# Dilated attention on tokens kept in another order, and the norm vector loaded first

## The chip, the cores and the metric

One core of a Trainium2 chip runs the program. The metric is the device time of one execution in microseconds (us); lower is better. Engines: TensorE (PE; PEld is its weight load), VectorE (DVE), ScalarE (ACT), GpSimd (POOL) and SyncE (SP, which issues most DMAs; POOL issues stores). Each engine works through its own instructions in order.

## The reference

Two residual layers on 1024 tokens of width 1024, in fp32. Layer 1 joins grouped-query attention and a neighbourhood attention; layer 2 joins a gated delta-rule branch and the dilated attention that the change is about. Cut to what matters there:

```python
DILATED_PATTERNS = ((128, 1), (512, 4), (2048, 16))      # window, dilation

def dilated_pattern(q, k, v, rel_bias, window, dilation):
    # query t attends to keys t - j*dilation, j = 0..window/dilation, causal:
    # positions are split into `dilation` residue classes; within one, blocks of 128
    # queries see their own block of keys and the one before it
    scores = einsum(qb, kw) + bias[bucket(distance)]
    lse = logsumexp(scores); p = exp(scores - lse)
    return einsum(p, vw), lse

def dilated_attention_branch(qkv, gate, ...):             # 8 heads of 64
    outs, lses = the three patterns, each over rms-normed q and k
    o = sum(softmax(stack(lses)) * stack(outs))            # the union
    return o * silu(gate)

mixed = concat([y_dn, y_att]); return x + mixed @ w_out
```

## The kernel before

**Layers and streams.** `share` (L464) weaves two streams into one program: a main stream (attention, delta rule) and a fill stream (projections, output projection), whose matmuls are to stand where the main stream waits. A scheduler then fixes the order on each engine. Projections and score matmuls are done with operands split into a high and a low part (`whi`/`wlo`, `hh`/`hl`, `qh`/`ql`), three or two matmuls for one product.

**Start.** SP loads the first weights, eight tiles of x (`xt`, L560, raised in priority by `XPR`) and the norm vector `g8` (L553). TensorE transposes `g8` first, then the x tiles; ScalarE squares each x tile (L568), and evacuates the transposes, scaled by the vector, as `hh` (L589), VectorE the rest as `hl` (L590). From these the first projection starts.

**The dilated branch.** The fill stream projects q and k, v and the gate of a pair of heads j (0 to 3) to DRAM: `c_d[j]`, `cv_d[j]` and a part of `g2_d` (`proj_c`), token by token in natural order. `prep_c(j)` (L1527) loads q and k back (`lqk`), normalizes, transposes, and leaves k and q in SBUF with one token a column (`da0` to `da2`, or `k2`, `qh`, `ql`): 64 rows by 1024 columns for each head. `tables_c(j)` (L1520) loads the bias and mask tables from `rb_d`, which holds each head's bias expanded (stored by L1095, DRAM to DRAM, with an outermost count of 8): a DMA for each head and pattern.

`jobs_c(j)` (L1579) has 24 items a pair. `item` (L1591) issues, for 128 queries and the pair's two heads: four score matmuls (128x256; columns of q are the weights, columns of k move), on VectorE the custom addition of the table with the row's minimum (L1607), on ScalarE the exponential (L1609), on TensorE transposes (`s<-ident,Pc`), a copy to `PTc` (L1620), the matmuls with v (`po<-vc,PTc`), and on VectorE the copy into the result tile (L1630): `Nst` for dilation 4 and 16, `N0` for dilation 1. The items' order is eight of dilation 4, eight of dilation 16, eight of dilation 1:

```python
yield item(slice(c + 512 * n, c + 512 * n + 509, 4), slice(c, c + 512 * n + 509, 4), ...)   # dilation 4
yield item(slice(c, c + 1017, 8), slice(c, c + 1017, 8), ...)                              # dilation 16, two classes a tile
yield item(slice(i * 128, (i + 1) * 128), slice(max(i - 1, 0) * 128, (i + 1) * 128), ...)  # dilation 1
```

So the columns of q and k are 4, 8 and 1 elements (of 4 bytes) apart. Results of the first two patterns go to DRAM (`n_d[j][0]`, `n_d[j][1]`, by POOL, L1643 and L1650), and come back in token order.

**The union.** After items 4 and 8 of dilation 1, `union` (L1670) loads both other patterns' results of 512 tokens (`N`, L1675), takes the minimum over the patterns (`M`, L1678, L1679), the weights (`W`, `D`), loads the gate (`gtc`, L1693), merges and gates (L1699 to L1703) and has POOL store the result to `o2_d` (L1707); for the last pair it stays in SBUF (`od3`). There are eight unions in all.

**The end.** `first_part(2)` in the fill stream multiplies the seven first groups of 128 columns of the mixed rows with `w_out` and keeps sums in `yp_d` (L945 to L950). The last group, pair 3's, is done in `fill2` (L1151): each of eight tiles of `od3` is transposed (`mth`, `mtl`), multiplied, added (L1172) to what `yp_d` holds and stored.

Of the kernel before, what the change touches and what calls it, by code (L numbers as in the profile page):

```python
# [153 lines left out]
def hybrid_kernel(ctx: ExitStack, tc: tile.TileContext, A, out, dbg=None, upto=99):  # L154
# [102 lines left out]
    def rows(t, i):  # L257
        return t[i * 128:(i + 1) * 128]
# [283 lines left out]
    rb_d = dp.tile([8, 128, 1024], F32, name="rb_d")  # L542

# [6 lines left out]
    with tc.tile_pool(name="xp", bufs=2, reuse_waits="tile") as xp:  # L550

        g8 = xp.tile([8, 128], F32, name="g8", bufs=1)
        ld(g8, dram(A["norm_gain"], 0, [[128, 8], [1, 128]]))  # L553
# [236 lines left out]


# [121 lines left out]
    def put_mixed(M, i, k0, n, od, gd, to=None, buf=e5):  # L913
        r = (slice(i * 128, i * 128 + 128), slice(k0 * 128, (k0 + n) * 128))
        ot = buf()[:, 0:n * 128]
        ld(ot, od[r])
# [22 lines left out]
    def first_part(b, od, gd, w, src, dst, mk):  # L939

        def part(ks, src):
# [11 lines left out]
            for i in range(NT):  # L953
                put_mixed(M_, i, ks[0], len(ks), od, gd if ks[0] == 0 else None, buf=buf)
                yield 0.43
# [7 lines left out]
        yield from part(range(4), src)  # L963
        last_w.extend(out_w(w, range(LASTC[b], 8), c) for c in range(2))
# [156 lines left out]
    ab_d = [dp.tile([64, 256], F32, name="ab_d%d" % k) for k in range(4)]  # L1121
    tb_d = [dp.tile([64, 256], F32, name="tb_d%d" % k) for k in range(4)]


    def proj_c(j):
        def evac(i, p):
            sg = e5()
            S.activation(sg[:, 0:384], p[:, 0:384], AF.Copy)
            st(rows(c_d[j], i), sg[:, 0:256])
            st(rows(cv_d[j], i), sg[:, 256:384])  # L1130
            gate_out(p[:, 384:512], g2_d[i * 128:(i + 1) * 128, 512 + j * 128:512 + (j + 1) * 128], sg[:, 384:512])

        yield from proj_tok(H[2], w2, [(2056 + 128 * j, 512, 4, 128)], evac)
# [17 lines left out]
    def fill2():  # L1151
# [14 lines left out]
        for i in range(NT):  # L1166
            x = xx[i // 2][:, i % 2]
# [7 lines left out]
            yield from wait(("c", 3, i // 4))  # L1175
            to = tuple(wk.tile([128, 1, 128], F32R, name=n, bufs=2) for n in ("mth", "mtl"))
            put(to, slice(0, 128), od3[i // 4][:, i % 4].rearrange("p h d -> p (h d)"), 0, 1, 0.5)
# [342 lines left out]
    def tables_c(j):  # L1520
        Ts = [wk.tile([128, 2, w], F32, name="tab%d" % k, bufs=2) for k, w in enumerate((256, 256, 128))]
        for h in range(2):
            for k, T in enumerate(Ts):
                ld(T[:, h], dram(rb_d, (2 * j + h) * 131072 + 384 * k + 128, [[1023, 128], [1, T.shape[2]]]))
        return Ts

    def prep_c(j):  # L1527
# [22 lines left out]
        X[j] = k2, qh, ql, tables_c(j) if j else None  # L1550
        for b in range(0, NT, 4):
            ssq = sm.tile([128, 4, 4], F32, name="ssc", bufs=2)
            qk = []
            for i in range(0, 4, 2):
                qk += [tmp("lqk", 2 * LQ)]
                ld(qk[-1], c_d[j][(b + i) * 128:(b + i + 2) * 128].rearrange("(t p) (h d) -> p t h d", p=128, d=64))
# [5 lines left out]
            for i in range(b, b + 4):  # L1562
# [14 lines left out]
                yield 0.54  # L1577

    def jobs_c(j):  # L1579
# [5 lines left out]
        def values(n, *ap):  # L1585

            v = tile_c("vc")
            ld(v.rearrange("p t h d -> p (t h d)").rearrange("p (a b) -> p a b", a=n), dram(cv_d[j], 0, list(ap)))
            return [v[:, t] for t in range(8)]

        def item(q, k, vs, T, N, then=None):  # L1591
# [7 lines left out]
            for h in range(2):  # L1599
                kk = k2[:, h, k] if nkt == 2 else k2[:, :, k]  # L1600
# [5 lines left out]
            for h in range(2):  # L1606
                V.tensor_tensor_reduce(out=P[:, h, :nk], in0=sh[h], in1=T[:, h, T.shape[2] - nk:], op0=OP.add, op1=OP.min,  # L1607
# [29 lines left out]


        vs = values(2, [512, 128], [512 * 128, 2], [1, 512])
        for c in range(4):  # L1640
            N = nst()
            for n in range(2):
                then = (lambda N=N, c=c: st(dram(n_d[j][0], c * 132, [[4 * 132, 128], [512 * 132, 2], [1, 132]]), N)) if n else None  # L1643
                yield item(slice(c + 512 * n, c + 512 * n + 509, 4), slice(c, c + 512 * n + 509, 4),
                           [vs[c], vs[4 + c]][:n + 1], Ts[1], N[:, n], then)
        vs = values(1, [1024, 128], [1, 1024])
        for c in range(8):
            if c % 2 == 0:
                N = nst()
            then = (lambda N=N, c=c: st(dram(n_d[j][1], (c - 1) * 132, [[8 * 132, 128], [132, 2], [1, 132]]), N)) if c % 2 else None  # L1650
            yield item(slice(c, c + 1017, 8), slice(c, c + 1017, 8), vs[c:c + 1], Ts[2], N[:, c % 2], then)
        N0 = wk.tile([128, NT, 132], F32, name="N0")
        vs = values(8, [128, 128], [128 * 128, 8], [1, 128])
# [7 lines left out]
        for i in range(NT):  # L1661
            yield item(slice(i * 128, (i + 1) * 128), slice(max(i - 1, 0) * 128, (i + 1) * 128), vs[max(i - 1, 0):i + 1],
                       Ts[0], N0[:, i], (lambda b=i // 4: last(b)) if i % 4 == 3 else None)
# [5 lines left out]
    def union_c(j):  # L1669
        def union(N0, b):  # L1670

            Ns = [N0[:, 4 * b:4 * b + 4]]
            for p in range(2):
                N = tile_c("N%d" % (p + 1))
                ld(N, n_d[j][p][512 * b:512 * b + 512].rearrange("(t p) c -> p t c", p=128))  # L1675
# [11 lines left out]
            for p in (1, 2):  # L1687
# [5 lines left out]
            ld(gt.rearrange("p t h d -> p t (h d)"),  # L1693
               g2_d[512 * b:512 * b + 512, 512 + j * 128:640 + j * 128].rearrange("(t p) c -> p t c", p=128))
# [12 lines left out]
            st(dram(o2_d, 4 * b * 128 * 1024 + 512 + j * 128, [[1024, 128], [128 * 1024, 4], [1, 128]]), od.rearrange("p t h d -> p t (h d)"))  # L1707
# [59 lines left out]
```

## Time and profile before

| | us |
|---|---|
| median of 3 runs (lowest to highest) | 1679.88 (1677.62 to 1684.44) |
| the profiled execution | 1676.17 |
| its span | 1674.4 |

The granted clock was 0.976 of full speed over the span. Times in the rows count from the start of the span. A row of the timeline has its start, its length, engine, line, operation, output from inputs, shapes, and how many instructions of one kind were drawn together; in brackets stands the idle time of the engine before it, and what ended it. The dilated stage runs from about 1335 to 1645, the last output tiles after that.

### The profile page before, as it was taken

The page shows a single profiled execution, that of the slowest core. Times are in us where ns is not written, and L with a number is a line of the kernel's source. Part 1 is how long each engine was busy: PE and PEld are TensorE (multiplying, and loading weights), DVE is VectorE, ACT ScalarE, POOL GpSimd, SP SyncE. Part 2 cuts the span into 40 slices and gives each one's busy share as a digit, 9 for nine tenths or more (in the row PEclk, how much of TensorE's full clock was granted, in tenths as well). Part 3 has the DMA queues.
Part 4 walks back from the last instruction along what each step waited for, and adds up shares of the span by engine and source line. Part 5 has one row for each costly group of instructions (what it writes and reads, how often), then busy time and mean ns, then how long its engine had stood idle before and what let it go on. Part 6 is the DMA issues. An engine that isn't in the chain of part 4 may idle for free. (4 is left out here: it accounts for less than half of the span.)

```text
span 1674.4 us, 27776 instructions
## 1 busy us (share of the span) xinstructions
PE 1529.0 (91%) x9363; PEld 1345.6 (80%) x9363; DVE 1108.9 (66%) x3401; ACT 780.7 (47%) x2196; POOL 262.3 (16%) x475
## 2 busy tenths in 40 slices
PE   2988999999999989996799999998999979999996
PEld 2877788989898878884677788887888868788984
DVE  5569866666665554568546768577677677957646
ACT  6246445455454443544344443444443354566631
POOL 0000111212122212111100102122212011111122
PEclk9999999999999899998899999999999989999999
DMA  6321112331215797775344423314222375633475
GB/s 168 118 63 53 53 63 90 80 99 54 95 47 150 241 273 212 226 231 142 82 102 107 99 83 89 95 52 110 79 79 73 113 222 170 193 93 90 134 246 208
DMA packets 165738, 208.47 MB, mean 125 GB/s; under 512 B 23435, under 2 KB 119371, under 8 KB 165596
## 3 DMA queue, kind: packets, MB, share of 16 engines
q1 hardware_dynamic: 138476, 131.35, 29.0%
q0 software_dynamic: 27120, 75.36, 13.1%
q8 instruction: 74, 1.21, 0.3%
q14 instruction: 68, 0.56, 0.1%
HBM read 135.51 MB, written 75.32 MB: 126 GB/s over the span
## 5 line engine op out<-in xcount | busy, mean ns | idle before, releaser
L172 PE MATMUL pw<-whi,hh 128*128 128x512 f32 (+2 forms) x1032 | 358.4, 349 | 8.6 <-ACT whi L353 2.5
L172 PE MATMUL pw<-wlo,hh 128*128 128x512 f32 (+2 forms) x1032 | 356.9, 346 | 0.9 <-DVE wlo L354 0.9
L172 PE MATMUL pw<-whi,hl 128*128 128x512 f32 (+2 forms) x1032 | 355.5, 345 | 0.0
L172 PEld LDWEIGHTS pw<-whi,hh 128*128 128x128 f32 x1032 | 196.4, 191 | 31.6 <-ACT whi L353 4.4
L172 PEld LDWEIGHTS pw<-wlo,hh 128*128 128x128 f32 x1032 | 197.0, 191 | 20.0 <-DVE wlo L354 1.3
L172 PEld LDWEIGHTS pw<-whi,hl 128*128 128x128 f32 x1032 | 196.6, 190 | 20.1
L354 DVE TENSOR_TENSOR wlo<-e,whi 128x512 fp32r<-128x512 f32 (+3 forms) x168 | 103.2, 624 | 57.1 <-ACT whi L353 56.7
L172 PE MATMUL pw<-hh,whi 128*128 128x512 f32 x320 | 128.7, 402 | 11.2 <-ACT whi L353 10.8
L353 ACT ACTIVATE whi<-e 128x512 fp32r<-128x512 f32 (+3 forms) x168 | 95.2, 581 | 74.9 <-DMA e<-in_w_in_dram 59.9
L172 PE MATMUL pw<-hl,whi 128*128 128x512 f32 x320 | 126.4, 396 | 0.0
L172 PE MATMUL pw<-hh,wlo 128*128 128x512 f32 x320 | 125.0, 399 | 0.0
L172 PE MATMUL s<-k,qT 128*128 128x512 f32 (+1 forms) x282 | 89.3, 396 | 3.2 <-DVE rq_t L285 1.6
L172 PE MATMUL po<-vc,PTc 128*128 128x128 f32 x560 | 82.8, 283 | 4.0 <-DVE N L1630 3.1
L1607 DVE CUSTOM_DVE_ANT_0 Pc<-s,tab 128x128 f32<-128x128 f32 (+1 forms) x192 | 59.7, 348 | 39.8 <-PE s L172 34.6
L172 PEld LDWEIGHTS po<-vc,PTc 128*128 128x128 f32 x560 | 75.6, 198 | 8.5 <-DVE N L1630 4.8
L172 PEld LDWEIGHTS pw<-hh,whi 128*128 128x128 f32 x320 | 60.6, 189 | 25.9 <-ACT whi L353 13.9
L172 PE MATMUL po<-PT,vv 128*128 128x256 f32 x512 | 75.2, 286 | 1.1 <-ACT PT L774 0.6
L766 ACT ACTIVATE P<-s,nm 128x512 f32<-128x512 f32 x77 | 52.5, 685 | 45.8 <-DVE nm L763 41.6
L172 PEld LDWEIGHTS po<-PT,vv 128*128 128x128 f32 x512 | 67.9, 190 | 5.2 <-ACT PT L774 1.7
L1609 ACT ACTIVATE Pc<-Pc,Nst 128x128 f32<-128x128 f32 (+1 forms) x128 | 53.6, 421 | 35.5 <-DVE Nst L1607 25.0
L172 PEld LDWEIGHTS pw<-hh,wlo 128*128 128x128 f32 x320 | 60.3, 189 | 11.8
L172 PEld LDWEIGHTS pw<-hl,whi 128*128 128x128 f32 x320 | 60.5, 189 | 11.4
(422 smaller groups left out, 3530.0 us busy)
## 6 DMA issues: line engine op xcount, KB each, us to landing
e<-in_w_in_dram SPq DMA_DIRECT2D x72, 256.0 KB, 3.3
bq_d<-e POOLq DMA_DIRECT2D x32, 256.0 KB, 2.5
qT<-bq_d SPq DMA_DIRECT2D x32, 256.0 KB, 5.4
e<-in_w_out_dram SPq DMA_DIRECT2D x32, 256.0 KB, 3.9
xp_d<-mx POOLq DMA_DIRECT2D x32, 256.0 KB, 4.4
yp_d<-e POOLq DMA_DIRECT2D x32, 256.0 KB, 2.7
e<-in_w_in_dram SPq DMA_DIRECT2D x32, 192.0 KB, 3.6
raw_d<-e POOLq DMA_DIRECT2D x24, 256.0 KB, 2.4
```

Of the source, the lines that this page charges most:

```text
L172: self.last = f(*a, **k).ins
L353: S.activation(hi[:, :n], raw[:, :n], AF.Copy)
L354: V.tensor_tensor(lo[:, :n], raw[:, :n], f32(hi[:, :n]), op=OP.subtract)
L766: S.activation(P[:, hf * 512:(hf + 1) * 512], ss[hf], AF.Exp, bias=nm[:, 2:3], accum_out=den[:, h, hf:hf + 1])
L1607: V.tensor_tensor_reduce(out=P[:, h, :nk], in0=sh[h], in1=T[:, h, T.shape[2] - nk:], op0=OP.add, op1=OP.min, scale=-1.0, scalar=3e38, accu ...
L1609: S.activation(P[:, h, :nk], P[:, h, :nk], AF.Exp, bias=N[:, 128 + h:129 + h], scale=-1.0, accum_out=N[:, 130 + h:131 + h])
```

## The change

1. The load of `g8` gets a higher priority than those of x.
2. `c_d`, `cv_d` and the gate (now `gc_d`, of its own) are stored in another order of tokens, by `places`: a token's column is found from its number modulo 8 and so on, so that dilation 4 has columns 2 apart, dilation 16 contiguous ones, and dilation 1 columns 8 apart. `prep_c` and v's loads follow.
3. Whatever crosses between the orders by DMA uses `eighths`: four DMAs of 32 partitions with a DRAM side of [2][16][n] in place of one of 128 partitions. It is used for N, the gate, v of dilation 1, and the stores of the union (`oc_d`, of its own, in place of `o2_d`). `put_mixed` reads a tile's three groups from `oc_d` with three loads. A store of `n_d[j][0]` has an outermost count of 2 too.
4. The tables' rows and columns have to follow the order: `places_table` loads them in pieces (4 for dilation 1, 2 for each of the others, for each head), with the rows permuted by the DMA, into `nat`, and ScalarE copies blocks of 128 columns with the columns permuted (six a head). For pair 0 it is done in layer 1, kept in `tp_d` and loaded in one DMA.
5. The last eight output tiles come in the order 0, 4, 1, 5 and so on, each transposed by a matmul with the identity, its columns permuted.

Its core:

```diff
+        with tc.high_priority(2 * XPR):
+            ld(g8, dram(A["norm_gain"], 0, [[128, 8], [1, 128]]))
...
+    def places_table(j, h, k, nat, T):
+        w = 128 if k == 2 else 256
+        ds = ((4, 2, 16), (2, 16, 4), (16, 4, 2))[k]
+        f = (1023, 1023 * ds[0], 1023 * ds[0] * ds[1])
+        src = (2 * j + h) * 131072 + 384 * k + 128
+        if k == 2:
+            for z in range(2):
+                ld(nat[z::2, 0:w], dram(rb_d, src + f[2] * z, [[f[0], 16], [f[1], 4], [1, w]]))
+        else:
+            m = 128 // ds[0]
+            for x in range(ds[0]):
+                ld(nat[m * x:m * x + m, 0:w], dram(rb_d, src + f[0] * x, [[f[1], ds[1]], [f[2], ds[2]], [1, w]]))
+        for b in range(w // 128):
+            x4 = nat[:, 128 * b:128 * b + 128].rearrange("p (z y x) -> p x y z", x=ds[0], y=ds[1])
+            for d in (b, b + 2)[:2 if k == 0 and b == 0 else 1]:
+                S.activation(T[:, 128 * d:128 * d + 128].rearrange("p (x y z) -> p x y z", x=ds[0], y=ds[1]), x4, AF.Copy)
...
+    def places(t, i):
+        r = t.shape[1]
+        return dram(t, ((i >> 2) + 2 * (i & 3)) * r, [[8 * r, 16], [128 * r, 8], [1, r]])
+
+    def eighths(t, b, n):
+        r = t.shape[1]
+        return [(slice(32 * e, 32 * e + 32), dram(t, (b + 128 * e) * r, [[512 * r, 2], [8 * r, 16], [1, n]])) for e in range(4)]
...
-                yield item(slice(c + 512 * n, c + 512 * n + 509, 4), slice(c, c + 512 * n + 509, 4),
-                           [vs[c], vs[4 + c]][:n + 1], Ts[1], N[:, n], then)
+                def k(x, c=c):
+                    return x[:, 256 * c:256 * c + 256].rearrange("p (s n) -> p n s", n=2)
+                yield item(slice(256 * c + n, 256 * c + n + 255, 2), k, vs[2 * c:2 * c + n + 1], Ts[1][:, :, 128 - 128 * n:], N[:, n], then)
...
-            yield item(slice(c, c + 1017, 8), slice(c, c + 1017, 8), vs[c:c + 1], Ts[2], N[:, c % 2], then)
+            yield item(slice(128 * c, 128 * c + 128), None, vs[c // 2 + c % 2 * 4:][:1], Ts[2], N[:, c % 2], then)
...
-            yield item(slice(i * 128, (i + 1) * 128), slice(max(i - 1, 0) * 128, (i + 1) * 128), vs[max(i - 1, 0):i + 1],
-                       Ts[0], N0[:, i], (lambda b=i // 4: last(b)) if i % 4 == 3 else None)
+            def k(x, ks=ks):
+                return x.rearrange("p (s r) -> p r s", r=8)[:, ks]
+            yield item(slice(r, r + 1017, 8), k, vs[ks] if r else vs[0:1], T, N0[:, r], (lambda b=r // 4: last(b)) if r % 4 == 3 else None)
...
-                ld(N, n_d[j][p][512 * b:512 * b + 512].rearrange("(t p) c -> p t c", p=128))
+                for ps_, src in eighths(n_d[j][p], 4 * b, 528):
+                    ld(N[ps_].rearrange("p t c -> p (t c)"), src)
```

In the changed code lines move by up to 76: the addition of L1607 stands in L1670, the load of N in L1750, the gate's in L1769, the merge in L1774 to L1778, the output tiles' additions in L1222.

Three places of the engines' order. The first is ScalarE at the start, `sqrow` being the squares of the x tiles, `hh` the evacuations and `whi` the cast of weights. Before:

```order
L568 ACTIVATE sqrow,ssx<-xt 128x1024 x8
L353 ACTIVATE whi<-e_187 128x512
L589 ACTIVATE hh<-s,gT 128x256
L589 ACTIVATE hh<-pw,gT 128x256
L589 ACTIVATE hh<-s,gT 128x256
L589 ACTIVATE hh<-pw,gT 128x256
```

After:

```order
L570 ACTIVATE sqrow,ssx<-xt 128x1024 x6
L591 ACTIVATE hh<-s,gT 128x256
L591 ACTIVATE hh<-pw,gT 128x256
L570 ACTIVATE sqrow,ssx<-xt 128x1024
L591 ACTIVATE hh<-s,gT 128x256 x2
L591 ACTIVATE hh<-pw,gT 128x256 x2
L570 ACTIVATE sqrow,ssx<-xt 128x1024
```

Two evacuations now stand ahead of the seventh square and four more ahead of the eighth. The second place is SP at the second union of head pair 0; `lqk` and `nat` there belong to the preparation of the next pair, `e` to the output projection. Before:

```order
L1556 DMA lqk<-c_d_465 128x2x256
L1675 DMA N_15579<-n_d_0_470 128x4x132
L1556 DMA lqk<-c_d_465 128x2x256
L347 DMA e_16546<-in_w_out_dram 128x512
L1675 DMA N_15581<-n_d_1_471 128x4x132
L347 DMA e_17218<-in_w_out_dram 128x512
L1693 DMA gtc<-g_d 128x4x128
```

After:

```order
L808 DMA nat<-rb_d 32x1x256 x4
L808 DMA nat<-rb_d 64x1x256 x2
L1750 DMA N_15655<-n_d_0_471 32x1x528 x4
L1750 DMA N_15660<-n_d_1_472 32x1x528 x4
L1769 DMA gtc<-gc_d_495 32x1x512 x4
L1616 DMA lqk<-c_d_466 128x2x256
L808 DMA nat<-rb_d 32x1x256 x4
L808 DMA nat<-rb_d 64x1x256 x2
```

Three DMAs with others between them became twelve in a row, with table pieces on both sides. The third place is VectorE at the last union; `e` are the fill's last sums, `mtl` the low part of an output tile's transpose, `hl` and `hh` its additions. Before:

```order
L1678 TENSOR_TENSOR M<-N_17779,N_18073 128x8
L1630 COPY N_17779<-po 128x128
L1679 TENSOR_TENSOR M<-M,N_18075 128x8
L1682 TENSOR_TENSOR W<-M,N_17779 128x8
L1682 TENSOR_TENSOR W<-M,N_18073 128x8
L1682 TENSOR_TENSOR W<-M,N_18075 128x8
L312 SCALAR_TENSOR_TENSOR mtl<-pw,mth 128x128
L1686 TENSOR_TENSOR D<-W,N_17779 128x8
```

After:

```order
L1777 TENSOR_TENSOR od_18322<-od_18322,N_18301 128x512
L977 TENSOR_TENSOR e_17693<-pw,e_17693 128x512
L1778 TENSOR_TENSOR od_18322<-od_18322,gtc 128x512
L977 TENSOR_TENSOR e_17707<-pw,e_17707 128x512
L977 TENSOR_TENSOR e_17721<-pw,e_17721 128x512
L977 TENSOR_TENSOR e_17735<-pw,e_17735 128x512
L977 TENSOR_TENSOR e_17749<-pw,e_17749 128x512
L1233 SCALAR_TENSOR_TENSOR mtl<-pw,mth 128x128
L1222 TENSOR_TENSOR hl<-pw,hl 128x512 x2
```

The union stood between the output tiles, behind the last of the fill's sums; it now stands among those sums, and all output tiles behind both.

## Rows read from the trace of the kernel before

**Rows 1.** The page's engines: busy us, share of the span, instructions.

```profile
PE 1529.0 (91%) x9363; PEld 1345.6 (80%) x9363; DVE 1108.9 (66%) x3401; ACT 780.7 (47%) x2196; POOL 262.3 (16%) x475
```

**Rows 2.** Windows; columns: length, busy by engine as named, clock, DMA share, GB/s.

```profile
core 0: us, PE busy (x) PEld busy (x) DVE busy (x) ACT busy (x) POOL busy (x), PEclk, DMA share, GB/s
0.00:30.00 30.00, 4.96 (x21) 4.17 (x21) 12.26 (x56) 15.56 (x30) 0.20 (x4) 1.00 0.82 195
...
1335.00:1645.00 310.00, 286.78 (x1717) 257.06 (x1716) 215.55 (x860) 169.39 (x584) 43.66 (x72) 0.97 0.52 166
...
1640.00:1674.00 34.00, 20.91 (x95) 13.66 (x93) 22.34 (x52) 3.04 (x10) 9.19 (x17) 0.97 0.62 221
```

**Rows 3.** Timeline of TensorE, score matmuls by four: dilation 4, 16, then 1.

```profile
1335.05 1.29 PE L172 MATMUL s<-da,da 128*128 128x256 f32 x4
...
1374.45 1.30 PE L172 MATMUL s<-da,da 128*128 128x256 f32 x4
...
1422.51 0.74 PE L172 MATMUL s<-da,da 128*128 128x256 f32 x4
...
1428.76 0.72 PE L172 MATMUL s<-da,da 128*128 128x256 f32 x4
```

**Rows 4.** Timeline of SyncE: the norm vector's load.

```profile
8.99 0.34 SPq L553 DMA_DIRECT2D g<-in_norm_gain_dram  x1
```

**Rows 5.** Timeline of TensorE at the start; in brackets: idle before, its end.

```profile
23.28 0.27 PE L172 MATMUL po<-ident,g 8*128 8x8 f32 x1 [4.09 <-DMA g<-in_norm_gain_dram]
...
32.56 1.09 PE L172 MATMUL s<-ident,xt 128*128 128x128 f32 x4 [7.96 <-DVE hl L590]
```

**Rows 6.** Timeline of ScalarE at the start.

```profile
24.71 1.06 ACT L568 ACTIVATE sqrow<-xt 128x1024 f32<-128x1024 f32 x1 [1.55 <-DMA xt<-in_x_dram]
...
26.28 0.45 ACT L589 ACTIVATE hh<-s,gT 128x256 fp32r<-128x256 f32 x1
```

**Rows 7.** Timeline of TensorE at the entry to the dilated stage.

```profile
1350.64 1.57 PE L172 MATMUL s<-ident,Pc 128*128 128x128 f32 x6 [6.55 <-ACT Pc L1609]
```

**Rows 8.** Timeline of VectorE at the entry to the dilated stage.

```profile
1342.63 0.69 DVE L920 TENSOR_TENSOR e<-e,e 128x512 f32<-128x512 f32 x1
...
1349.28 0.28 DVE L1607 CUSTOM_DVE_ANT_0 Pc<-s,tab 128x128 f32<-128x128 f32 x1
```

**Rows 9.** Timeline of VectorE in the tail.

```profile
1639.85 0.69 DVE L949 TENSOR_TENSOR e<-pw,e 128x512 f32<-128x512 f32 x1 [1.67 <-PE pw L172]
...
1648.72 0.17 DVE L1678 TENSOR_TENSOR M<-N,N 128x8 f32<-128x8 f32 x1 [1.09 <-DMA N<-n_d]
...
1657.45 0.69 DVE L1703 TENSOR_TENSOR od<-od,gtc 128x512 f32<-128x512 f32 x1
...
1668.04 1.40 DVE L1172 TENSOR_TENSOR hh<-pw,hh 128x512 f32<-128x512 f32 x2 [0.80 <-PE pw L172]
```

**Rows 10.** Line L1273 on ScalarE: ns min/median/max.

```profile
L1273 ACT ACTIVATE sq_d<-orr x32: 292/310/356, 1037.3 to 1343.1; 128x128 f32<-128x128 f32 x32
```

**Rows 11.** DMA issues from 1335 to 1645: count, KB each, median us to landing.

```profile
vc<-cv_d SPq DMA_DIRECT2D x12, 512.0 KB, 4.2
...
N<-n_d SPq DMA_DIRECT2D x16, 264.0 KB, 3.5
...
tab<-rb_d SPq DMA_DIRECT2D x16, 128.0 KB, 3.1
gtc<-g_d SPq DMA_DIRECT2D x8, 256.0 KB, 3.4
```

**Rows 12.** The tile N: ns that SyncE takes to issue a load.

```profile
L1675 SPq DMA_DIRECT2D N<-n_d x16: 360/370/387, 1379.7 to 1643.3; - x16
```

**Rows 13.** Window with the store of the expanded tables (L1095) alone; columns as rows 2.

```profile
62.00:66.00 4.00, 4.00 (x35) 4.00 (x35) 3.35 (x20) 0.83 (x3) 0.00 (x0) 1.00 0.53 216
```

**Rows 14.** Waits between 1354 and 1590: us in total, times, longest.

```profile
DVE M L1679 <- DMA N<-n_d: 6.0, 4, 2.1
```

More of the change, by code (lines that the diff above doesn't have):

```diff
@@ L542, in hybrid_kernel @@
     rb_d = dp.tile([8, 128, 1024], F32, name="rb_d")
+    tp_d = dp.tile([128, 2, 768], F32, name="tp_d")
     w1 = A["w_in"][0]
@@ L915, in put_mixed @@
         ot = buf()[:, 0:n * 128]
-        ld(ot, od[r])
+        if isinstance(od, list):
+            for k, t in enumerate(od):
+                ld(ot[:, k * 128:k * 128 + 128], places(t, i))
+        else:
+            ld(ot, od[r])
         if gd is not None:
@@ L963, in first_part @@
         yield from part(range(4), src)
+        if b == 1:
+            for h in range(2):
+                for k, (a, z) in enumerate(COLS):
+                    nat, T = (wr.tile([128, w], F32, name=n, bufs=2) for n, w in (("nat", 256), ("tabp", 384)))
+                    places_table(0, h, k, nat, T)
+                    st(tp_d[:, h, a:z], T[:, 0:z - a])
         last_w.extend(out_w(w, range(LASTC[b], 8), c) for c in range(2))
@@ L1165, in fill2 @@
         xx = [wn.tile([128, 2, 1024], F32, name="hh" if k % 2 else "hl", bufs=2) for k in range(4)]
-        for i in range(NT):
-            x = xx[i // 2][:, i % 2]
+        for r in range(NT):
+            i = (r >> 1) + 4 * (r & 1)
+            x = xx[r // 2][:, r % 2]
             ld(x, rows(yp_d, i))
@@ L1173, in ev2 @@
                 st(out[i * 128:(i + 1) * 128, c * 512:c * 512 + 512], y)
-            yield from wait(("c", 3, i // 4))
+            yield from wait(("c", 3, r // 4))
             to = tuple(wk.tile([128, 1, 128], F32R, name=n, bufs=2) for n in ("mth", "mtl"))
-            put(to, slice(0, 128), od3[i // 4][:, i % 4].rearrange("p h d -> p (h d)"), 0, 1, 0.5)
+            tb = wbank()
+            PE.matmul(tb[:, 0:128], od3[r // 4][:, r % 4].rearrange("p h d -> p (h d)"), ident.rearrange("p (e c a) -> p a c e", e=4, c=2),
+                      start=True, stop=True)
+            hv, lv = (t[:, 0] for t in to)
+            S.activation(hv, tb[:, 0:128], AF.Copy, scale=0.5)
+            V.scalar_tensor_tensor(lv, tb[:, 0:128], 0.5, f32(hv), op0=OP.mult, op1=OP.subtract)
             yield 0.22
@@ L1520, in tables_c @@
     def tables_c(j):
[L1521 to L1525, printed above, removed]
+        T = wk.tile([128, 2, 768], F32, name="tab", bufs=2)
+        if j == 0:
+            ld(T, tp_d)
+        else:
+            nat = wk.tile([128, 2, 640], F32, name="nat")
+            for h in range(2):
+                for k, (a, b) in enumerate(COLS):
+                    places_table(j, h, k, nat[:, h, 256 * k:], T[:, h, a:b])
+        return [T[:, :, a:b] for a, b in COLS]
     def prep_c(j):
@@ L1606, in item @@
             for h in range(2):
-                V.tensor_tensor_reduce(out=P[:, h, :nk], in0=sh[h], in1=T[:, h, T.shape[2] - nk:], op0=OP.add, op1=OP.min,
+                V.tensor_tensor_reduce(out=P[:, h, :nk], in0=sh[h], in1=T[:, h], op0=OP.add, op1=OP.min,
                                        scale=-1.0, scalar=3e38, accum_out=N[:, 128 + h:129 + h])
@@ L1636, in nst @@
             return tile_c("Nst")
-        vs = values(2, [512, 128], [512 * 128, 2], [1, 512])
+        vs = values(4, *[(slice(64 * e, 64 * e + 64), dram(cv_d[j], 512 * e * 128, [[256, 64], [128 * 128, 4], [1, 256]])) for e in range(2)])
         for c in range(4):
@@ L1706, in union @@
                 return
[L1707 removed]
+            for ps_, dst in eighths(oc_d[j], 4 * b, 512):
+                st(dst, od[ps_].rearrange("p t h d -> p (t h d)"))
         return union
```

41 lines of the change are left out of this document (24 added, 17 removed).

## The prediction

> **What bounds the kernel now.** I read the page's table of engines first: TensorE is busy 1529.0 us of 1674.4, VectorE 1108.9 [rows 1]. So what the change does to TensorE counts nearly in full, and other engines' work counts only where TensorE stands still. Next the windows, because the edits lie in three stretches [rows 2]: in the first 30 us TensorE does 4.96 us of work; in the dilated stage, 1335 to 1645, it does 286.78 of 310.00 us, the granted clock is 0.97 and the DMA engines are 0.52 busy; from 1640 to the end it does 20.91 of 34.00. The stage therefore moves with TensorE's own work, the two ends with their chains of waits. The sum is made against the profiled execution, 1676.17 us, which is 3.7 below the median of the runs, 1679.88. About 0.5%, 8.4 us, is what a measurement can tell from no change, so the marks are 1671.5 and 1688.3.
>
> **Score matmuls with other strides.** An item issues four score matmuls of 128x256. With columns a stride of 4 or 8 apart the group of four takes 1.29 and 1.30 us, with contiguous columns 0.74 and 0.72 [rows 3]. A stride of 4 is 16 bytes, one of 8 is 32: they cost the same. There are 8 items of each pattern in each of 4 head pairs, so 32 groups a pattern. Before: 32 contiguous, 32 at stride 4, 32 at stride 8. After: 32 at stride 8, 32 at stride 2, 32 contiguous. So two of the three classes trade places, and the whole gain hangs on the price of stride 2, 8 bytes, which the trace of before does not show. Its bounds are the two rows: 1.29, gain 0; 0.72, gain 32 x 0.57 = 18.2 us. I take the lower price, since 8 bytes is nearer to 4 than to the 16 at which the dear price has already been reached. TensorE is busy 93% of the stage [rows 2], and a shorter matmul gives its time only where the next one's data are there, but the fill's matmuls stand between the items: **-18**, ends -18.2 and 0. The Trainium skill (SBUF — State Buffer, Specifications) says lines of SBUF are 16 bytes and want two hits each for full bandwidth. By it stride 2 (two hits) would have the low price and stride 4 (one) the high one; the rows on strides 4 and 8 agree, and no row shows stride 2.
>
> **The norm vector first.** SP issues g at 8.99, behind the eight x loads [rows 4]; TensorE's first instruction waits 4.09 us for it [rows 5], and all transposes stand behind it. ScalarE then makes the last tile's square at 24.71, after a wait of 1.55 for that tile, and the first evacuation only at 26.28 [rows 6]. After the change g is ahead of the x loads, and six of the sixteen first evacuations stand ahead of the eighth square. Gain: the wait of 4.09 less what then waits for x instead; the evacuations can fill the 1.55 and what ScalarE lost to the late start. I take **-3.5**; ends 0 (the x tiles, 0.82 of the DMA engines' time in this window [rows 2], are late anyway) and -8, the 7.96 us that TensorE later stands for VectorE [rows 5].
>
> **Entry to the dilated stage.** TensorE stands 6.55 us until the first items' exponentials come [rows 7]; VectorE reaches the first of its additions at 1349.28, and at 1342.63 it still does fill work of 0.69 us a piece [rows 8], four pieces until then. In the new order that work stands earlier, and pair 0's table comes in one load, from rows that layer 1 prepared, in place of six. Three of the pieces lie on the chain: **-2**; ends 0 and -6.5.
>
> **The tail.** Before, the fill's last addition is at 1639.85, the second union of pair 3 waits for its loads at 1648.72, ends with the gate at 1657.45, and four output tiles follow, the last at 1668.04 [rows 9]: some 29 us, of which TensorE works 20.91 in the window of 34.00 [rows 2]. After, the union's merge and gate stand among the fill's last nine additions, four of them behind the gate, so its chain runs beside fill matmuls, and the eight tiles come in one run. The tiles' pace is 2.5 us: from the gate, 1657.45, to the end of the last addition, 1668.04 + 1.40, are 12.0 us, of which 2.0 go to the gate itself and an earlier pair of additions, and the other 10 to four tiles. Eight tiles and some 4 us before them make 24: **-5**; ends 0 and -8. The new transposes (a matmul by a permuted identity) have the shape of the old ones and are costed at nothing.
>
> **Tables on ScalarE.** Pairs 1 to 3 load their tables in natural row order and ScalarE copies 128x128 blocks with permuted columns: 12 a pair, 36 in the stage. The nearest row is an activation of 128x128 at 0.31 us [rows 10]: 36 x 0.31 = 11 us. ScalarE has room, but the copies come in bursts (up to 11 in a row in its order) between exponentials for which TensorE waits; a burst of 11 is 3.4 us. Three pairs with about 1.3 each that is not covered: **+4**; ends 0 and +11. The 12 copies in layer 1 lie beside projections, at nothing; without that cover they would add 12 x 0.31 = 4.
>
> **Loads that few DMA engines carry.** N comes in 64 DMAs of 66 KB in place of 16 of 264, the gate in 32 of 64 KB in place of 8 of 256, the third pattern's v in 16 of 128 KB in place of 4 of 512; one quarter of the tables in four pieces [rows 11]. SP issues some 129 DMAs more from the first table load on, at 0.37 us each [rows 12], 48 us of its queue over 310, which has that room. The rows get longer (2112 bytes in place of 528), so fewer packets. Against that, the DRAM side of each such DMA has an outermost count of 2. The trace has a store whose outermost count is 8: while it runs alone, the DMA engines are 0.53 busy at 216 GB/s [rows 13], that is half of the 16, at 216 / (16 x 0.53) = 25.5 GB/s each. If the outermost count sets how many engines work, two carry 51 GB/s. The Trainium skill (DMA: Bandwidth & Descriptors, Why a DMA increments its semaphore by 16 and not by 1) says so: the count of engines is the largest number up to 16 that divides both sides' slowest dimension. The row of the store with 8 agrees; no row shows a count of 2.
> Worked out for a pair: N 16 x 67.6 KB = 1081, gate 524, v 524, tables 262, together 2.39 MB; at 51 GB/s 47 us in the 78 us that a pair lasts (about 310 / 4). That fits, if the queue is not asked all at once. It is asked at a union: N 541 KB and gate 262 take 10.6 + 5.1 = 16 us instead of some 6 (two landings of 3.5 and 3.4 [rows 11] with their issues). VectorE now waits 6.0 us in four waits at the minimum over N [rows 14]; I take about one us more at each of the eight unions: **+9**. Ends: -6 (the waits go) and +40 (rival A). The stores of N and of the results go through POOL, whose queue the 24 result stores lengthen by 18; nobody waits for those but the late out-projection, so nothing.
>
> **Sum.** -18 - 3.5 - 2 - 5 + 4 + 9 = -15.5: 1676.17 - 15.5 = 1660.7, and with the 3.7 to the median 1664.4; I say **1665**, own range 1655 to 1675.
>
> **Rivals.**
> A, slower: the two engines become the bound. Place: the minimum over N at the second union of each pair, on VectorE, with the copies and additions of the next pair's items queued behind it and TensorE waiting for those. Price: the full 16 - 6 = 10 us at each of 4 second unions, 40, in place of my 9, so 31 more, of which some 4 in the last pair fall beside fill matmuls: 1665 + 27 = 1692. It decides if VectorE reaches the minimum less than 16 us after N's first load could start. For it: outermost count 2 in the diff, 0.53 in the row with count 8, and SP's order, where both N, the gate and table pieces follow each other. Against it: the 0.52 of DMA time in the stage leaves the queue room, and the four waits at the minimum come to only 6.0 us now. By the rule of the Trainium skill named above (DMA: Bandwidth & Descriptors) two engines it would be. Chance 0.20.
> B, the few engines cost nothing: the loads of four pieces spread, rows of 2112 bytes go faster than those of 528, and the waits at N vanish. In place of +9 about -2: 1654. For it: only 0.52 of the DMA time is used. Against it: the row with count 8. Chance 0.20.
> C, the change does not do what it says to the matmuls: stride 2 is as dear as stride 4, and the -18 is 0: 1665 + 18 = 1683, say 1682. For it: strides of 4 and 8 don't differ, so it may be contiguous or not that counts. Chance 0.15.
>
> **How the numbers follow.** Forecast 0.45, A 0.20, B 0.20, C 0.15. Faster by over 0.5%: four fifths of the forecast (0.36) and all of B, 0.55 in round numbers; within: the rest of the forecast, nearly all of C and a little of A, 0.25; slower: most of A, 0.20. The range runs from 1647, which holds most of B (1654 with some us below for a start at its end of -8), to 1692, the middle of A: left out are half of A and a third of B at most, under 0.2.
>
> **What would show it.** In the profile of the changed kernel: score groups of the dilation-16 pattern 0.72, of dilation 4 0.72 (C: 1.29), of dilation 1 1.29; TensorE's first instruction before 20 us; N's landing 3 to 5 us (A: 10 or more) and the waits at the minimum over N under 20 us in sum (A: 40). If the dilated stage is not some 10 us shorter while TensorE's work in it has fallen by 18, the loads or the bursts on ScalarE ate it, and the prediction's two added terms are too small. If TensorE's work has not fallen, it is the price of stride 2.

## The result, and the profile after

The changed kernel takes 1796.38 us (median of 4 runs, 1793.74 to 1802.39) against 1682.16 of the kernel before on the same chip: ratio 1.0671, 95% interval 1.0644 to 1.0698, some 114 us slower. The forecast of 1665 us and its whole range are wrong; the sign too. Below, differences in us between runs are differences of their ratios to the kernel before, times its 1684 us.

The page's engines and the windows of the kernel after (columns as in [rows 2]):

```profile
PE 1567.8 (87%) x9371; PEld 1374.7 (77%) x9371; DVE 1107.8 (62%) x3401; ACT 798.0 (44%) x2244; POOL 280.0 (16%) x499
...
0.00:30.00 30.00, 7.23 (x29) 5.56 (x29) 13.20 (x57) 17.39 (x34) 0.20 (x4) 1.00 0.82 194
```

```profile
1367.00:1797.00 430.00, 321.64 (x1748) 277.73 (x1748) 222.15 (x854) 178.94 (x610) 65.50 (x105) 0.88 0.39 124
...
1686.00:1689.00 3.00, 0.00 (x0) 0.00 (x0) 0.00 (x0) 0.00 (x0) 0.00 (x0) 0.50 0.13 52
1689.00:1692.00 3.00, 0.00 (x0) 0.00 (x0) 0.00 (x0) 0.00 (x0) 0.00 (x0) 0.50 0.13 52
```

From the first exponential's transposes to the end it takes 430 us where the kernel before took 324 (1350.64 [rows 7] to its span's end, 1674.4), with nearly as many instructions and a granted clock of 0.88. That is 106 us; some 17 more in these two profiles lie before it. The last two rows show what happens: no compute engine works, the clock has gone down to its lower level of 1.2 GHz, and the DMA engines are 0.13 busy at 52 GB/s. 0.13 of 16 is two engines. The timeline of TensorE and that of SyncE at that place, and long waits after 1330 (columns as in [rows 14]; the last two rows are the kernel before):

```profile
1694.91 0.48 PE L172 MATMUL pw<-ident,e 128*128 128x128 f32 x1 [13.62 <-DMA e<-oc_d]
```

```profile
1676.18 3.58 SPq L1651 DMA_DIRECT2D vc<-cv_d  x4
1679.94 2.45 SPq L942 DMA_DIRECT2D e<-oc_d  x2
1682.53 3.83 SPq L1750 DMA_DIRECT2D N<-n_d  x2
1695.42 0.56 SPq L942 DMA_DIRECT2D e<-oc_d  x1
```

```profile
PE pw L172 <- DMA e<-oc_d: 24.3, 4, 13.6
...
DVE M L1753 <- DMA N<-n_d: 18.2, 4, 6.1
...
DVE M L1754 <- DMA N<-n_d: 13.3, 4, 5.0
...
DVE M L1679 <- DMA N<-n_d: 8.2, 6, 2.1
DVE M L1678 <- DMA N<-n_d: 1.1, 1, 1.1
```

The waits at the minimum over N, 9.3 us before (6.0 of them in the window of [rows 14]), are 31.5 now. The single longest, 13.62, is for a load of `oc_d` whose own outermost count is 16, the first of the two issued from 1679.94 on: it lands late in a stretch in which two engines work off a backlog.

The trace also keeps every update of the semaphore that counts a load's landing. A load of N in the kernel before has sixteen. In the changed kernel it has one, 1.0 us after its issue, and then two, for example both at 3.5 us (issue at 1382.61); in the run runs16b below, where its outermost count is 8, it has one and then eight. So with an outermost count of 2 or 8 as many engines report. N lands after 6.1 us in the median, 13.8 at most; before it was 3.5. The load of `oc_d` issued at 1679.94 has sixteen updates: fourteen between 2.5 and 2.9 us, the other two only at 14.5 and 14.9. So TensorE stood for two of its sixteen engines.

The score matmuls after, by four, of dilation 4, 16 and 1 (against [rows 3]):

```profile
1376.68 1.17 PE L172 MATMUL s<-da,da 128*128 128x256 f32 x4
...
1397.28 0.72 PE L172 MATMUL s<-da,da 128*128 128x256 f32 x4
...
1411.13 1.29 PE L172 MATMUL s<-da,da 128*128 128x256 f32 x4
```

Dilation 16 and 1 changed places as forecast, but stride 2, now dilation 4's, costs 1.17, not 0.72.

### The profile page after: what moved, and what is told of

Same layout as the page of the kernel before. It is cut to its first block, busy times and chain, and to the rows that moved or that the text cites. A ratio compares the mean times of both kernels' runs of the same rounds, so it can differ in the third digit from the quotient of the medians.

```text
span 1796.7 us, 28066 instructions
## 1 busy us (share of the span) xinstructions
PE 1567.8 (87%) x9371; PEld 1374.7 (77%) x9371; DVE 1107.8 (62%) x3401; ACT 798.0 (44%) x2244; POOL 280.0 (16%) x499
## 4 chain that ended last, share of the span: by engine, by line
issue 37%; PE 27%; DMA 19%; POOL 7%; DVE 5%; ACT 2%; SPq 1%; POOLq 0%; DVEq 0%; ACTq 0%
PE pw L172 17%; PE s L172 6%; DMA n_d<-Nst 3%; DMA N<-n_d 3%; PE po L172 2%; DMA e<-oc_d 2%; DMA gtc<-gc_d 2%; PE p L172 2%; POOL g_d L524 1%; DMA e<-in_w_in_dram 1%; DMA nat<-rb_d 1%; DMA e<-in_w_out_dram 1%; POOL o_d L648 1%; DMA e<-yp_d 1%; DMA xt<-in_x_dram 1%
## 5 line engine op out<-in xcount | busy, mean ns | idle before, releaser
L172 PE MATMUL pw<-whi,hh 128*128 128x512 f32 (+2 forms) x1032 | 363.2, 353 | 12.5 <-DVE e L977 7.0
L172 PE MATMUL pw<-wlo,hh 128*128 128x512 f32 (+2 forms) x1032 | 361.0, 350 | 0.1
L172 PEld LDWEIGHTS pw<-whi,hh 128*128 128x128 f32 x1032 | 200.2, 195 | 35.6 <-DVE e L977 7.7
L172 PEld LDWEIGHTS pw<-whi,hl 128*128 128x128 f32 x1032 | 200.3, 194 | 20.6
L172 PEld LDWEIGHTS pw<-wlo,hh 128*128 128x128 f32 x1032 | 200.7, 194 | 19.9 <-DVE wlo L354 0.6
L172 PE MATMUL po<-vc,PTc 128*128 128x128 f32 x560 | 91.8, 304 | 28.0 <-DVE Nst L1693 13.7
L172 PEld LDWEIGHTS po<-vc,PTc 128*128 128x128 f32 x560 | 83.3, 216 | 34.1 <-DVE Nst L1693 15.9
L172 PE MATMUL s<-ident,Pc 128*128 128x128 f32 x280 | 62.1, 309 | 30.5 <-ACT Pc L1672 29.9
L1670 DVE CUSTOM_DVE_ANT_0 Pc<-s,tab 128x128 f32<-128x128 f32 (+1 forms) x192 | 59.3, 348 | 40.5 <-PE s L172 29.6
L172 PEld LDWEIGHTS s<-ident,Pc 128*128 128x128 f32 x280 | 40.6, 159 | 39.6 <-ACT Pc L1672 36.8
```

Of the source, the lines that this page charges most:

```text
L172: self.last = f(*a, **k).ins
```

## The experiments

**Engines or the number of DMAs.** Two runs on the changed kernel.

```diff
-        return [(slice(32 * e, 32 * e + 32), dram(t, (b + 128 * e) * r, [[512 * r, 2], [8 * r, 16], [1, n]])) for e in range(4)]
+        return [(slice(32 * e, 32 * e + 32), dram(t, (b + 256 * e) * r, [[8 * r, 32], [1, n]])) for e in range(4)]   # four16
...
+        return [(slice(0, 128), dram(t, b * r, [[8 * r, 128], [1, n]]))]                                           # one16
```

> Two theories for the 114 us that the change added. Engines: a DMA whose DRAM side has an outermost count of 2 runs on two engines, so N, the gate, v and the results land late. Queue: it is the number of DMAs on SyncE, each 0.6 us to issue and, by the waits of SyncE in the changed kernel (8.5 us on a load of the same tile), held until an earlier one has landed. Here the four DMAs stay four, with the same bytes and row lengths, but their DRAM side is one run of 32 strided rows instead of 2 times 16 (other rows than the right ones, so the merged values are of the wrong tokens). Engines: below 1715. Queue: 1780 to 1800, no change.

> One DMA of 128 partitions in place of the four, for N, the gate, v and the results (again rows of other tokens). Engines: the same as with four DMAs on many engines, within 5 us. Queue: here, and only here, the time falls, to below 1715. Both theories leave some 10 to 30 us over the kernel before, for the tables and the results' loads.

Measured: 1.0173 (1.0138 to 1.0209) and 1.016 (1.012 to 1.0199). Four DMAs with the same bytes, but an outermost count of 32, take away 84 of the 114 us, and one in place of four adds nothing to that that can be told. The engines, then: in four16 a load of N has sixteen updates of its semaphore, and lands after 2.4 us in the median. SyncE's side of it, the tile N in the kernel after, in four16 and in one16 (ns to issue one load, min/median/max):

```profile
L1750 SPq DMA_DIRECT2D N<-n_d x64: 583/616/2172, 1382.6 to 1732.1; - x64
```

```profile
L1750 SPq DMA_DIRECT2D N<-n_d x64: 302/419/1512, 1381.8 to 1652.7; - x64
```

```profile
L1750 SPq DMA_DIRECT2D N<-n_d x16: 319/325/402, 1404.1 to 1666.7; - x16
```

Even the issue of a DMA with an outermost count of 2 is longer, 616 ns against 419.

**The tables, alone and with that.**

```diff
-                    places_table(j, h, k, nat[:, h, 256 * k:], T[:, h, a:b])
+                ld(T[:, h, a:b], dram(rb_d, (2 * j + h) * 131072 + 384 * k + 128, [[1023, 128], [1, b - a]]))
```

> The changed kernel with the tables loaded as before, six DMAs a pair, no copies on ScalarE and none of the preparation in layer 1 (the table's rows and columns are then in the wrong order). Engines: 36 of the 64 pieces are of two engines, 32 KB each, and the 48 copies take 0.43 us each: 10 to 20 us less, 1775 to 1785. Queue: 40 DMAs fewer at 0.6 us, and what is queued behind them: 25 to 40 less, 1755 to 1770. If the tables cost nothing: 1790 to 1800.

> The two edits of the earlier runs together: one DMA for N, the gate, v and the results, and the tables as before. If the costs add, 1710 - 16 = 1694, some 10 over the kernel before. If the tables' 16 us were mostly their two-engine pieces' place in SyncE's queue, which one16 has already relieved, more than 1700.

Measured: 1.0571 (1.053 to 1.0612), 17 us less than the changed kernel; with one16, 1.0103 (1.0062 to 1.0144), 10 less than one16. By the intervals each difference is known to some 8 to 10 us, so that the two may be the same. In the profiles about half of it lies in the stage, counted from the first exponential's transposes to the end: 429.3 us against 421.6 without these tables, and 349.3 against 340.1 with one16. Part of the rest lies in layer 1, where the changed kernel prepares pair 0's tables and ScalarE waits for their pieces (columns as in [rows 14], between 590 and 660):

```profile
ACT tabp L813 <- DMA nat<-rb_d: 24.4, 5, 10.2
```

TensorE's 3700th to 3900th matmuls, which are issued there, take 40 to 46 us in the four profiles of kernels with this preparation (after, four16, one16, fix16), and 34 to 37 in those without it, the kernel before among them. (Of the pieces, 32 have an outermost count of 2, not the 36 of the expectation.)

**The stores of dilation 4's results.** The prediction had put them at nothing.

```diff
-  st(dram(n_d[j][0], 128 * c * 132, [[512 * 132, 2], [2 * 132, 64], [1, 264]]), N.rearrange("p n c -> p (n c)"))
+  [st(dram(n_d[j][0], (128 * c + 512 * e) * 132, [[2 * 132, 64], [1, 264]]), N[64 * e:64 * e + 64]...) for e in range(2)]
```

> As one16_plain, and the stores of dilation 4's results, which still have an outermost count of 2, split into two DMAs of 64 partitions with one run of 64 rows each, on POOL's queue. Their landing is 5.9 us in the changed kernel, 3.2 before. Engines: those stores land in about 3 us and the time is 3 to 8 us below one16_plain, at the level of the kernel before (1684) or just under. If the loads of N no longer wait for these stores: the same as one16_plain.

Measured: 0.9978 (0.9957 to 1.0). 21 us came from 16 stores on POOL, more than the 3 to 8 that were expected of them. Landing of these stores alone, min/median/max, in the kernel after and in this run:

```profile
DMA to landing us min/median/max: 5.6/6.7/8.4
```

```profile
DMA to landing us min/median/max: 1.9/2.8/3.7
```

VectorE's addition writes the row's minimum into a buffer of `Nst`, and has to wait until the store of that buffer's last results has landed. In one16_plain (columns as in [rows 14]):

```profile
DVE Pc L1660 <- DMA n_d<-Nst: 13.6, 7, 3.2
```

In one16_plain_st and in the kernel before there is no such wait. SyncE's wait for these stores, in front of the loads of N, falls by 9 more, from 29.9 to 20.5 us.

Taken out in this order, the parts account for the whole loss: 86 us N, gate, v and results, 10 tables, 21 stores are 117, and what is left of the change is 4 us faster than the kernel before, at the edge of its interval.

**Backlog over the stage, or a price at each place.** Part of the two-engine transfers put back into one16_plain_st: N alone, and the gate, v and the stores of the merged results without N.

```diff
-                for ps_, src in eighths(n_d[j][p], 4 * b, 528):     # n_two
+                for ps_, src in twos(n_d[j][p], 4 * b, 528):
...
+            for ps_, src in twos(gc_d[j], 4 * b, 512):              # rest_two; v and the results' stores likewise
```

> one16_plain_st (1678), with the loads of N alone put back into four DMAs of outermost count 2 (the rows the changed kernel reads). Theory backlog: the two engines also carry a sixteenth each of every other load, 0.52 x 310 = 161 us of the stage; N adds 4 x 1.08 MB at 51 GB/s = 85 us, together 246 of 310, so they don't saturate and the time rises by little, under 20 us, at the unions alone. In the changed kernel N, the gate, v and table pieces add 188 us and the two engines would need 349, more than the stage has, which is where the 84 us came from. Theory proportional: each byte on two engines costs the same wherever, N being half of those bytes: 84 x 0.5 = 42 us more, 1720.

> one16_plain_st with the gate's and v's loads and the stores of the merged results alone put back into outermost count 2, N staying in one DMA. Backlog: 4 x 1.05 MB at 51 GB/s = 82 us, again 243 of 310: under 20 us more, and n_two and rest_two together well under 84. Proportional: 42 us more, 1720, and the two together 84.

Measured: 1.0237 (1.0194 to 1.0281) and 1.027 (1.0227 to 1.0314), 44 and 49 us over one16_plain_st. Together 93, no less than the 86 that both cost in one: the theory of a backlog over the stage, by which half of the bytes would have fitted, falls. The price arises in bursts, at each place where a transfer is waited for. Waits in one16_plain_st and in rest_two, TensorE for the load of `oc_d`, which has an outermost count of 16 in both:

```profile
PE pw L172 <- DMA e<-oc_d: 1.0, 4, 0.4
```

```profile
PE pw L172 <- DMA e<-oc_d: 14.9, 3, 12.4
```

A load on all engines is held up by transfers on two: it is done when its last share is, and two of its sixteen shares come late. The load of `oc_d` issued at 1571.54 in rest_two has fourteen updates of its semaphore by 2.8 us and the last two at 14.4 and 14.8; in one16_plain_st no such load takes more than 4.8. The stores to `oc_d` are slower in rest_two too, but this load was issued when they had landed, so they don't explain these 12 us. The Trainium skill (DMA: Bandwidth & Descriptors, Why a DMA increments its semaphore by 16 and not by 1) has such loads always on the lowest-numbered engines, so that several of them don't spread; the 0.13 with more than one of them outstanding and the two late shares agree, though no row names the engines.

**What strides cost, and whose.**

```diff
-  yield item(slice(c + 512 * n, c + 512 * n + 509, 4), slice(c, c + 512 * n + 509, 4), ...)
+  yield item(slice(c + 512 * n, c + 512 * n + 509, 4), slice(128 * c, 128 * c + 128 * (n + 1)), ...)
...
-  yield item(slice(c, c + 1017, 8), slice(c, c + 1017, 8), ...)
+  yield item(slice(128 * c, 128 * c + 128), slice(c, c + 1017, 8), ...)
```

> The kernel before, with the strides taken apart: in the items of dilation 4 the keys (the moving side, 256 columns) are read contiguously and the queries (the weights, 128 columns) at stride 4; in those of dilation 16 the queries contiguously and the keys at stride 8 (other columns than the right ones, so the scores are of the wrong tokens). Theory moving: the keys' stride sets the price, so groups of dilation 4 take 0.72 to 0.75 us and those of dilation 16 stay at 1.29; 32 groups less by 0.57 each, up to 18 us less. Theory weights: the reverse, dilation 4 at 1.29 and dilation 16 at 0.72. If either stride is enough for the high price: all 1.29, no change of the time.

Groups of dilation 4 (queries strided, keys contiguous), then of dilation 16 (the reverse):

```profile
1361.23 1.19 PE L172 MATMUL s<-da,da 128*128 128x256 f32 x4
```

```profile
1372.16 1.11 PE L172 MATMUL s<-da,da 128*128 128x256 f32 x4
```

Neither the moving side nor the weights alone set the price; nearest comes the third case. One strided side already brings the group to 1.1 or 1.2, both to 1.29. The time was 0.998 (0.9958 to 1.0001), not clear of no change.

**What a shorter score matmul is worth.** The kernel before with both sides contiguous in all patterns.

```diff
+  yield item(slice(128 * c + 512 * n, 128 * c + 512 * n + 128), slice(128 * c, 128 * c + 128 * (n + 1)), ...)
...
+  yield item(slice(128 * c, 128 * c + 128), slice(128 * c, 128 * c + 128), ...)
```

> The kernel before with queries and keys of all three patterns read contiguously (other columns than the right ones for dilation 4 and 16, so the scores are of the wrong tokens) and nothing else changed: TensorE gets 64 x 0.57 = 36 us less to do, with no copy, table or load to pay for it. The prediction took such work as almost wholly on the path, because TensorE is busy 93% of the stage: then 1684 - 36 = about 1650. Rival: the items' chain through the other engines sets much of the stage; one half strided gave 3.4 us of 11: then a third, 12 us less, 1672.

Measured: 0.9935 (0.9911 to 0.9959), 11 us of 36. TensorE's score matmuls of `da` from 1345 or 1350 on, all_contiguous and the kernel before (busy us, mean ns):

```profile
L172 PE MATMUL s<-da,da 128*128 128x256 f32 x180 | 34.0, 312 | 2.6 <-ACT PTc L1620 2.5
```

```profile
L172 PE MATMUL s<-da,da 128*128 128x256 f32 x180 | 48.4, 400 | 2.2 <-ACT PTc L1620 1.9
```

The matmuls did get shorter. The windows of the last 1740 matmuls, the kernel before and all_contiguous (columns as in [rows 2]):

```profile
1350.64:1674.40 323.76, 296.71 (x1740) 261.37 (x1740) 220.79 (x852) 165.89 (x572) 51.88 (x88) 0.97 0.51 165
```

```profile
1354.21:1666.60 312.39, 274.90 (x1740) 234.00 (x1740) 219.44 (x852) 165.75 (x572) 51.89 (x88) 0.96 0.54 170
```

By the trace's own records the score matmuls in them take 32 us less (100.9 to 68.8), but the others 8 more, and TensorE's busy time falls by 22. Half of that, 10 us, became idle time, and 11 reached the time.

**The norm vector alone, on the kernel before.**

```diff
-        ld(g8, dram(A["norm_gain"], 0, [[128, 8], [1, 128]]))
+        with tc.high_priority(2 * XPR):
+            ld(g8, dram(A["norm_gain"], 0, [[128, 8], [1, 128]]))
```

> The kernel before with the load of the norm vector ahead of those of x and nothing else changed. The prediction had 3.5 us less for it, 0.2%. The trace of the changed kernel has the first projection matmul at 45.85 in place of 45.40, so the rival is no difference: within 1 us.

Measured: 1.0009 (0.9986 to 1.0031). No difference.

**The changed kernel with every transfer on 16 engines.** fix16_plain is the same with the tables loaded as in plain_tables.

```diff
-        return [(slice(32 * e, 32 * e + 32), dram(t, (b + 128 * e) * r, [[512 * r, 2], [8 * r, 16], [1, n]])) for e in range(4)]
+        return [(slice(16 * e, 16 * e + 16), dram(t, (b + 128 * (e // 2) + 512 * (e % 2)) * r, [[8 * r, 16], [1, n]])) for e in range(8)]
...
+                    for y in range(2):
+                        ld(nat[m * x + 16 * y:m * x + 16 * y + 16, 0:w], dram(rb_d, src + f[0] * x + f[1] * y, [[f[2], 16], [1, w]]))
```

> The changed kernel, computing the same, with every transfer that had an outermost count of 2 split so that it has 16 or 64: N, the gate, v and the results' stores in eight DMAs of 16 partitions in place of four of 32, the dilation-4 results' store in two of 64, the eight table pieces of a pair with a count of 2 in sixteen of 16 partitions. It doubles those DMAs and moves the same bytes. Engines: the 84 and 22 us go, and of the tables' 10 to 16 the part that is not ScalarE's copies: 1680 to 1695. Queue: twice as many DMAs on SyncE, over 1720.

> fix16 (1705) with the tables as before, six DMAs a pair and no copies (in the wrong order of rows and columns). It differs from one16_plain_st (1678) then only in N, the gate, v and the results going in eight DMAs of 16 partitions in place of one. If the tables make what fix16 has left: 1680 to 1686. If the number of DMAs has a price of its own: more, up to 1700.

The store of dilation 4's results is split as in one16_plain_st. Measured: 1.0108 (1.009 to 1.0127), above what was expected of the engines alone, and 1.0064 (1.0043 to 1.0085). Twice as many DMAs, all on 16 engines, and 95 of the 114 us are gone; fix16 computes the same as the changed kernel, so this doesn't hang on wrong rows. What is left, 18 us, is in part the tables (7) and in part the eight DMAs for one (14 over one16_plain_st): 128 loads of N of 16 partitions where 16 of 128 stood have a price after all, a small one. Whether it is their number or their size wasn't tested.

**Contiguous reads in another order of tokens.** Two versions: tokens in eight classes, keys read in runs, queries copied by ScalarE into contiguous order. The core of it:

```diff
+        return dram(t, 16 * i * r, [[r, 16], [128 * r, 8], [1, r]])                      # places: column = 128 * (token % 8) + token // 8
...
+                u = wk.tile([128, 2, 1024], F32R, name="qs%d" % m, bufs=1)               # queries for dilation 4, then 1
+                for h in range(2):
+                    S.activation(out(u[:, h]), view(f32(t[:, h])), AF.Copy)
...
+                return t.rearrange("p (b i a) -> p i b a", b=8, i=8)[:, i - 1:i + 1]     # keys of dilation 1: runs of 16 columns
```

> A version of its own: tokens in eight classes modulo 8, 128 columns each, natural order within. Keys are then read in runs of 128, 64 and 16 contiguous columns for dilation 16, 4 and 1. [...] Every load and store has 8 or 16 as its outermost count. The items go four of dilation 16, dilation 4, four of dilation 16, dilation 1. If runs of 16 columns cost what contiguous columns cost, all 96 groups of score matmuls take 0.72 and TensorE has 64 x 0.57 = 36 us less work than in the kernel before: 1650 to 1665, the copies and a tighter supply of buffers costing some of it. If short runs cost as strides do, dilation 1 stays at 1.1 and the time is 1670 to 1690.

> runs16 in the items' old order (dilation 4, 16, 1), v loaded three times a pair as before instead of four, and the queries' copies kept in two halves of 512 columns, each made while other items run. In runs16 SyncE stood 51 us for v's buffers and with it the loads of the next pair's queries and keys. If that was what ate the 36 us that TensorE's score matmuls gave: 1655 to 1675. If it is the chain of the items itself (sum, exponential, transpose, copy) that TensorE then waits for: 1690 to 1710.

Measured: 1.0164 (1.0126 to 1.0203), 1713 us and above both forecasts, and 1.0081 (1.0056 to 1.0106): no version beats the kernel before. A group of dilation 1 in runs16, and a part of ScalarE's copies there, 16 of 32 (busy us, mean ns):

```profile
1425.17 0.73 PE L172 MATMUL s<-da,qs 128*128 128x256 f32 x4
```

```profile
L1706 ACT ACTIVATE qs<-da 128x1024 fp32r<-128x1024 f32 x16 | 15.6, 1045 | 0.1
```

Runs of 16 columns cost what contiguous ones do. But those reads are worth 11 us (all_contiguous), and 32 us of copies stand on the engine that also makes the exponentials. runs16b gains 14 us on runs16 by three edits at once (the old order of items, v loaded three times, copies in halves), so none of them is shown to be the cause. What the rest is stays open as well: the items' chain was argued, and N comes there in 64 loads that eight engines carry (landing 2.7 us in the median), which no run took out.

## Why the prediction was wrong

**Loads that few engines carry (+9, rival A +40): the step that failed.** Its mechanism was right: 0.13 of 16 engines at 52 GB/s, where the prediction had worked out 51 for two, and two engines that report for a load of N. The count of engines that the Trainium skill gives (the page and section named above) agrees. What failed is the size. The prediction had a union's loads 10 us longer, 16 instead of 6, and let "about one us more at each of the eight unions" of that reach the time, since 47 us of transfer fit into the 78 us of a pair and VectorE waits little there before. But the queue is asked all at once, eight times for N and the gate, four times for v, and somebody waits each time; v and the results' stores had no term at all. N takes 541 KB at 51 GB/s, 10.6 us, where 16 engines take 1.3: eight unions make 74 us more, and n_two shows 44 of them. The gate (8 x 4.5), v (4 x 9.0) and the results (6 x 4.5) make 99, and rest_two shows 49. About half of the transfers' lengthening came onto the path, not the sixteenth that +9 was of 74 + 36 + 36; with what they hold up, the place measured 86 us (the changed kernel against one16). Rival A named place and engine count, but let only the second unions pay, and left out v and the stores too.

**Stores through POOL "nobody waits for": wrong by 21 us.** VectorE waits for them to get the buffer back, 13.6 us in one16_plain, and N's load waits for them, on SyncE, in front of everything else in its queue (`DMA n_d<-Nst` there: 21.0 us before, 64.3 in the kernel after, with the backlog in it). And the load is itself waited for at the union.

**Stride 2 (-18): rival C was nearly right, and the term was mis-sized besides.** Stride 2 costs 1.17 against 1.29. Dilation 1 and 16 trade 0.72 and 1.29, and only dilation 4 gains: 32 x 0.12 = 4 us of TensorE. The Trainium skill (SBUF — State Buffer, Specifications), by which two hits on a line would give full bandwidth, does not hold for these operands: 1.17 is near the dear end. And had it been 0.72, a third of it would have reached the time if all_contiguous is the measure, about 6 us: TensorE's busy share of 93% does not say that less work on it is less time.

**The norm vector (-3.5): no gain** (gain_first). The mechanism worked, the first evacuation came at 20.69 instead of 26.28, but the first projection matmul at 45.85 instead of 45.40. TensorE now stands for the x tiles, which VectorE scales, instead (timeline of TensorE in the kernel after):

```profile
23.22 0.47 PE L172 MATMUL s<-ident,xt 128*128 128x128 f32 x1 [4.53 <-DVE xt L572]
```

It had 4.09 for g before [rows 5]: the wait changed its name, as the end at 0 had it.

**The entry (-2): no gain.** TensorE stands 6.91 us there, 6.55 before [rows 7]:

```profile
1367.40 0.90 PE L172 MATMUL s<-ident,Pc 128*128 128x128 f32 x3 [6.91 <-ACT Pc L1672]
```

**The tail (-5): right.** From the fill's last addition to the end of the last output's, 1768.12 to 1790.93, are 22.8 us (24.9 in one16_plain_st); before, 1639.85 to 1669.44, 29.6 [rows 9].

```profile
1768.12 0.69 DVE L977 TENSOR_TENSOR e<-pw,e 128x512 f32<-128x512 f32 x1 [1.94 <-DMA e<-yp_d]
...
1789.54 1.39 DVE L1222 TENSOR_TENSOR hh<-pw,hh 128x512 f32<-128x512 f32 x2 [0.73 <-PE pw L172]
```

Of the four gains it alone shows in full: the sum had 28.5 us of them, and one16_plain_st, with the dear transfers and tables taken out, shows 4.

**Tables (+4): 7 to 17, by the run.** The prediction had put the preparation in layer 1 at nothing, and part of the price lies there. A copy with permuted columns takes 0.44 us, not 0.31, 36 times on ScalarE in the stage (line L813, ns min/median/max):

```profile
L813 ACT ACTIVATE tab<-nat x36: 407/438/464, 1374.2 to 1567.8; 128x128 f32<-128x128 f32 x36
```

**The clock.** The stage's 0.88 against 0.97 [rows 2] goes with TensorE's standing, and in one16_plain_st, between 1350 and the end, it is 0.98. It is not free: with nearly the same instructions TensorE is busy 321.64 us in the changed kernel and 296.71 before, so 25 of the stage's 106 us are matmuls that took longer. No run separates this from the waits that bring it.

## What to carry to other kernels

Look at the outermost count of a DMA's DRAM side before its bytes: 2 there meant two engines of 16 and about 52 GB/s, and late landings for what was queued with it. Price a lengthened transfer at every place where somebody waits for it, store to buffer and store to load to use; in this kernel about half of the lengthening became time. That it fits into the stage's sum is no comfort. And before work is taken from the busiest engine, try what a kernel gains that leaves the work out: here TensorE was busy 93% and 11 us of 36 came through.

## What was not expected of the hardware

Four fp32r score matmuls of 128x256 take 0.72 us with both operands contiguous, 1.11 to 1.19 with either one strided, 1.17 with both at stride 2, and 1.29 with both at stride 4 or 8; a moving operand in runs of 16 columns costs as little as a contiguous one (0.73). SyncE takes 616 ns to issue a DMA of 32 partitions with an outermost count of 2, and 419 with one of 32 (medians). A load on sixteen engines beside transfers on two has fourteen engines done at 2.9 us and the last two at 14.9.
